# Where the matmul operands begin in SBUF: padded weight slots in a two-layer streaming encoder

## The chip, the cores and the metric

The kernel runs on one NeuronCore of one Trainium2 chip. The metric is the device time of one execution in microseconds. Before the change three runs took 1301.45, 1302.26 and 1303.33 us; the median is 1302.26. The profile is of one further execution, which took 1301.85 us; its span from the first to the last instruction is 1300.1 us, and 1.75 us lie around that span.

## The reference

A sequence of 512 frames with 1024 features goes through two layers. Layer 0 mixes with an RWKV-7 recurrence beside attention into 256 memory tokens; layer 1 mixes with chunked attention beside memory attention. Each mixer is followed by an output projection and by a gated feed-forward block with a short convolution. All arithmetic is float32.

```python
def conv_glu(h, w_in, conv_w, conv_b, w_out):        # D_FF = 2816, CONV_W = 3
    seq = h.shape[1]
    gate, val = jnp.split(h @ w_in, 2, axis=-1)
    gp = jnp.pad(gate, ((0, 0), (CONV_W - 1, 0), (0, 0)))
    conv = conv_b + sum(conv_w[j] * gp[:, j:j + seq] for j in range(CONV_W))
    return (jax.nn.gelu(conv, approximate=False) * val) @ w_out

for layer in range(DEPTH):                            # DEPTH = 2
    h = rms_norm(x, ln1[layer])
    p = h @ w_in_of_the_layer
    mix = rwkv7_time_mix(...) if layer == 0 else chunk_attention(...)
    mo = memory_attention(q_mem, mem_n, w_mem_kv[layer])
    x = x + jnp.concatenate([mix, mo], axis=-1) @ w_out[layer]
    x = x + conv_glu(rms_norm(x, ln2[layer]), ffn_in[layer], ffn_conv[layer],
                     ffn_conv_b[layer], ffn_out[layer])
return rms_norm(x, ln_f)
```

## The kernel before

**Products.** Every large product is made of three matmuls on float32r operands. A float32 operand is split into a high part (a copy rounded to float32r, on ScalarE, ACT) and a low part (the remainder, a subtraction on VectorE, DVE, or a negated copy on ACT with a DMA that adds the source, issued by GpSimd, POOL). The three are high by high, high by low, and low by high. Each matmul has 128 stationary columns ("weights") and a moving operand of 512 or of 256 columns, and each brings its own weight load.

**Weight slots.** The pool `wp` holds raw weights (`wraw`, 2 slots), high parts (`whi`, 3 slots) and low parts (`wlo`, 3 slots), each 1024 float32 columns a partition, 4096 bytes. `split_w`, `raw_w` and `load_w` (L172 to L198) fill them. `wlv` is one more low part that shares the slots of `wraw`.

**512-wide products.** `dense` (L213) has the weights in `whi`/`wlo` and a 512-wide activation moving: `r1h`/`r1l` in layer 0's projections, in layer 0's output projection, in layer 1's key projections (`k_proj`) and in the last tile of layer 1's feed-forward input; `r2h`/`r2l` in the corresponding places of the other layer. `rows` (L652, matmuls on L658 and L663) computes the feed-forward output with the activations stationary (`r1h`, `r1l`, `r2h`, `r2l`, `th`, `tl`, `sl`) and the 512-wide chunks of `whi`/`wlo` moving.

**256-wide products.** The feed-forward input projection takes 21 of its 22 tiles by a seven-product scheme on half-size blocks: class `Seven`, one `frame` (L506) a tile, whose seven calls of `prod` (L408, matmuls on L414 and L416) make 7 x 12 = 84 matmuls, each with a 256-wide moving operand out of `Uh`/`Ul` (3 products) or `Th`/`Tl` (4 products) and weights out of `whi`, `wlo` or `wlv`. `U` is `r2h`/`r2l` in layer 0 and `r1h`/`r1l` in layer 1; `T` is `th`/`tl` in both. While PE works on tile j, DVE and ACT build the sums and splits of tile j + 1 and finish tiles j - 1 and j - 2. Inside the frames every DVE and ACT instruction stands in a written order (`keep`). `v_proj` (L1711) has 256-wide weights moving and `r1h`/`r1l` stationary.

**The order around them.** In the mixer stages generators of instructions are woven by cost (`weave`, L87); the feed-forward stages are written out by hand. The tile framework adds all waits: a new tile in a slot waits for the last reader of the old one.

**Places.** The allocator puts tiles of a pool one behind the other and rounds each up to 32 bytes. `cst` begins 16,512 bytes into a partition; it has 710 columns (2840 bytes, rounded to 2848), `vec` 316 columns (1264, rounded to 1280), and `r1h` follows at 20,640. This gives, in the built program, as bytes past a multiple of 256:

| tiles | bytes past a multiple of 256 |
|---|---|
| `r1h`, `r1l`, `acc`, `rho` | 160 |
| `wraw`, `wlv`, `whi`, `wlo` (all slots), `tmp` | 128 |
| `r2h`, `r2l`, `th`, `tl`, `sl`, `raw`, `sp`, `xT` | 128 |

Inside these tiles an operand begins at a multiple of 512 bytes (128 weight columns) or of 1024 or 2048 (256 or 512 moving columns), so an operand has the place of its tile.

Of the kernel before, what the change touches and what calls it, by code (L numbers as in the profile page):

```python
# [112 lines left out]
        e[3] = now + wait  # L113


@with_exitstack
def trunk_kernel(ctx, tc, A, out):
    nc = tc.nc
# [1 line left out]
    cp = ctx.enter_context(tc.tile_pool(name="cp", bufs=1))  # L120
    wp = ctx.enter_context(tc.tile_pool(name="wp", bufs=3))
    dp = ctx.enter_context(tc.tile_pool(name="dp", bufs=1, space=bass.MemoryType.DRAM))
    banks = {}

    def open_banks(stack, **n):
# [3 lines left out]

    open_banks(ctx, D=2)  # L130
    cst = cp.tile([P, NCST], F32, name="cst")
    vec = cp.tile([P, NVEC], F32, name="vec")
    r1h = cp.tile([P, KD, S], F32R, name="r1h", tag="r1h")
    r1l = cp.tile([P, KD, S], F32R, name="r1l", tag="r1l")
    acc = cp.tile([P, S], F32, name="acc")
    rho = cp.tile([P, S], F32, name="rho")
    rc = cp.tile([P, 4], F32, name="rc")

    def C(name, lo=0, n=None):
        o, w = COFF[name]  # L140
# [28 lines left out]
    lo_on = [0]  # L169
    raw_at = [None]  # L170

    def split_w(raw, n, src=None, pin=lambda i: i, first=False, hold=False):  # L172
        hi = wp.tile([P, 1024], F32R, name="whi", tag="whi")
        lo = wp.tile([P, 1024], F32R, name="wlo", tag="wlo")
        high = lambda: pin(SC.copy(hi[:, :n], raw))  # L175

        def low():
            if src is not None:

                pin(SC.activation(lo[:, :n], raw, AF.Copy, scale=-1.0))  # L180
                GP.dma_start(lo[:, :n], src, accum_op=ALU.add)
            else:
                pin(V.tensor_tensor(lo[:, :n], raw, hi[:, :n], op=ALU.subtract))  # L183

        first, second = (low, high) if first else (high, low)
        first()
        if hold:
            return hi, lo, second
        second()
        return hi, lo  # L190

    def raw_w(src, n=1024):
        raw = wp.tile([P, 1024], F32, name="wraw", tag="wraw", bufs=2)
        raw_at[0] = nc.sync.dma_start(raw[:, :n], src)
        return raw[:, :n]

    def load_w(src, n=1024, lo=None):
        return split_w(raw_w(src, n), n, src if (lo_on[0] if lo is None else lo) else None)  # L198

    def mm3(ps, wh, wl, ah, al, start, stop):  # L200
        PE.matmul(ps, wh, ah, start=start, stop=False)
# [195 lines left out]
    def ffn(l, hp, U, T, new_x, xT, after=None, tokens=None):  # L397
# [29 lines left out]
        class Seven:  # L427
# [18 lines left out]
                    GP.dma_start(low[:], self.second[:, n], accum_op=ALU.add)  # L446

            def rest(self):
                self.low = wp.tile([P, 1024], F32R, name="wlv", tag="wraw", bufs=2)
                keep(SC.activation(self.low[:], self.pair(G2), AF.Copy, scale=-1.0))  # L450
                GP.dma_start(self.low[:].rearrange("p (a s) -> p a s", a=2), self.second, accum_op=ALU.add)  # L451

# [11 lines left out]
                keep(V.tensor_tensor(raw[:, S4], raw[:, S2], raw[:, G2], op=ALU.add))  # L464

            def high(self, what, n=1024):
                hi = wp.tile([P, 1024], F32R, name="whi", tag="whi")
                keep(SC.copy(hi[:, :n], self.pair(what) if n > S else self.raw[:, what]))  # L468
                return hi

            def lower(self, what, hi, n=1024):
                lo = wp.tile([P, 1024], F32R, name="wlo", tag="wlo")
                keep(V.tensor_tensor(lo[:, :n], self.pair(what) if n > S else self.raw[:, what], hi[:, :n], op=ALU.subtract))  # L473
                return hi, lo

# [30 lines left out]
            def frame(self, prev2, prev, nxt, norm=None, ending=None):  # L506
                first = prev is None
                if nxt:
                    nxt.load()
                f1, f2, f3, self.f4 = (ps_f() for _ in range(4))  # L510
                g = self.g = tmp()
                prod(f1[:, h1], (self.gs, 0), XU(0, 0))
                if first:
                    hv = self.hv
                    self.h31 = self.high(S3)
                else:
                    hv = self.high(G2)
                keep(SC.copy(g[:, h1], f1[:, h1]))
                if first:
                    prod(self.f4[:, h1], ((hv, self.lows[0]), 0), XU(1, 0), True)  # L520
                if norm and not first:
                    run(norm)
                w31 = self.lower(S3, self.h31)
                if prev:
                    prev.end1()
                    prev.endr()
                prod(f2[:, h1], (self.gs, S), XT(T2), first)
                w4 = self.lower(S4, self.high(S4, S), S)
                if nxt and prev:
                    prev.end2()  # L530
                    prev.endt()
                elif prev:
                    next(ending)
                    next(ending)
                keep(V.tensor_tensor(g[:, h2], g[:, h1], f2[:, h1], op=ALU.subtract))  # L535
                if nxt and prev:
                    prev.end3()
                    prev.endd()
                if nxt:
                    nxt.sums()  # L540
                    nxt.sum2()
                    nxt.rest()
                if nxt and prev2:
                    prev2.end4()
                    prev2.end5()
                c = self.c = tmp()
                prod(f1[:, h2], (w31, 0), XT(T3))
                keep(V.tensor_tensor(c[:, h1], f1[:, h2], g[:, h2], op=ALU.subtract))
                if first:
                    next(norm)  # L550
                prod(f3[:, h2], (w31, S), XT(T1))
                if nxt:
                    nxt.gs = nxt.lower(G1, nxt.high(G1))
                    nxt.sum4()
                else:
                    next(ending)
                if first:
                    next(norm)
                v = self.v = tmp()
                prod(f3[:, h1], ((hv, self.lows[1]), S, 0) if first else ((hv, self.low), S), XT(T4))  # L560
                keep(V.tensor_tensor(v[:].rearrange("p (a s) -> p a s", a=2), c[:, h1].unsqueeze(1).to_broadcast([P, 2, 256]),
                                     f3[:].rearrange("p (a s) -> p a s", a=2), op=ALU.add))
                keep(V.tensor_tensor(g[:, h2], g[:, h2], f3[:, h2], op=ALU.subtract))
                if nxt:
                    nxt.h31 = nxt.high(S3)
                else:
                    next(ending)
                if not first:
                    prod(self.f4[:, h1], ((hv, self.low), 0), XU(1, 0))
                prod(self.f4[:, h2], (w4, 0), XU(1, 1))  # L570
# [69 lines left out]
        def chunk(raw, c, spare=False):  # L640
            n = 2 if c < 3 else 1
            s_ = raw[:, 2 * c:2 * c + n].rearrange("p k s -> p (k s)")
            if spare and c > 1:
                hi, lo = (t[:, 2 * c - 4:2 * c - 4 + n].rearrange("p k s -> p (k s)") for t in (Th, Tl))
            else:
                hi = wp.tile([P, 1024], F32R, name="whi", tag="whi")[:, :n * S]
                lo = wp.tile([P, 1024], F32R, name="wlo", tag="wlo")[:, :n * S]
            SC.copy(hi, s_)  # L648
            V.tensor_tensor(lo, s_, hi, op=ALU.subtract)  # L649
            return hi, lo, n  # L650
# [233 lines left out]
        return ap.unsqueeze(1).to_broadcast([P, 8, 64])  # L884

    def lora_load(idx):
        raw = wp.tile([P, 1024], F32, name="wraw", tag="wraw", bufs=2)
        nc.sync.dma_start(raw[:], A["lora"][idx])
        return raw

# [2 lines left out]
    xs = [Tt3[:, 0:2].rearrange("p m c t -> p m (c t)"),  # L893
          kt_("MQ", (P, 8, 128))[:].rearrange("p a b -> p (a b)").rearrange("p (m s) -> p m s", m=2)]
    xs += [flat(kt_("AR", (P, NCH, 2, 64), bufs=2), 2) for _ in range(2)]
    lraw = wp.tile([P, 1024], F32, name="wraw", tag="wraw", bufs=2)
    for m in range(KD):
        nc.sync.dma_start(xs[m // 2][:, m % 2], A["xT"][:, m])
        if m in (0, 2):
            u = slice(m * 256, m * 256 + 512)  # L900
            nc.sync.dma_start(lraw[:, u], A["lora"][0][:, u])
    nc.sync.dma_start(vec[:, 24:], A["vec"][:, 24:])
    kraw = wp.tile([P, 1024], F32, name="wraw", tag="wraw", bufs=2)
    nc.sync.dma_start(kraw[:], A["wA"][1])
    nc.sync.dma_start(cst, A["cst"])

# [13 lines left out]

    def lora_split(idx, raw, parts=1):

        hi, lo = zip(*((wp.tile([P, 1024], F32R, name="whi", tag="whi"), wp.tile([P, 1024], F32R, name="wlo", tag="wlo"))
                       for _ in range(2)))
        mraw = flat(kt_("KB", (P, NCH, 3, 64), bufs=2), 1)[:, 0, 0:1024]
        r3 = raw[:].rearrange("p (k f) -> p k f", k=8)
        m3 = mraw.rearrange("p (k f) -> p k f", k=8)
# [565 lines left out]
    def lora_one():  # L1493

        with tc.issue_after(norm_at[0].ins):
            *_, lw_ = lora_split(1, lora_load(1))
        yield from lora_pair(1, *lw_)


    lora0 = lora_pair(0, *lw)  # L1500
# [6 lines left out]
    GP.memset(acc[:], 1.0)  # L1507
    GP.memset(acc[:, 0:S:64], 0.0)
    run(lora0)
    first = prepare(0, Ts[0])  # L1510
    for _ in range(5):
        next(first)
# [130 lines left out]
    with ExitStack() as bctx:  # L1643
# [67 lines left out]
        def v_proj(g, wv=None):  # L1711
            yield lambda: g < 2 or 2 * g - 3 in done
            vS[g] = ap_.tile([P, 4, 256], F32, name="vS", tag="vS")
            wv = wv or [load_w(A["w_kvv"][g, u]) for u in range(2)]
            for t2 in range(2):

                pp_ = ps_d() if g else ps_s()
# [77 lines left out]
        run(dense(pq[1][:], [(first[1], K8)], act2, order=K8[4:8], start=False))  # L1795
        next(norm)
        run(dense(pk[:], [(wk, K8)], act1, order=K8[4:8], start=False))
        wv = [load_w(A["w_kvv"][0, u]) for u in range(2)]
        run(norm)
        for i in range(2):  # L1800
            q_split(pq[i], Tb[i])
# [187 lines left out]
```

## Time and profile before

| | us | share of the span |
|---|---|---|
| median of three runs | 1302.26 | |
| profiled execution | 1301.85 | |
| its span | 1300.1 | |
| PE busy (10,420 matmuls) | 1278.6 | 98% |
| PEld busy (weight loads) | 1100.9 | 85% |
| ACT busy | 836.5 | 64% |
| POOL busy | 137.6 | 11% |

The stages follow one another: layer 0's mixer up to about 388 us, the feed-forward frames of layer 0 from 388 to 603 us, its output from 613 to 727, layer 1's mixer from 727 to 953, the frames of layer 1 from 953 to 1166, its output from 1177 to the end. Matmuls are pipelined and their ends are modelled, so neighbouring matmuls overlap in the profile and the busy share of PE says little; the distance between the starts of two neighbours says what one costs. The chain of waits merges neighbouring matmuls of one line into a piece, with their count and the time from the first start to the start of what follows, and so shows this distance.

### The profile page before, as it was taken

What the parts mean: (1) busy time and instruction counts of PE and PEld (TensorE: products, weight loads), DVE (VectorE), ACT (ScalarE), POOL (GpSimd) and SP (SyncE); (2) the same over time, 40 slices, a digit from 0 to 9 for tenths busy, and PEclk for the clock granted to TensorE, in tenths of its full rate; (3) what the DMA queues carried; (4) which work ended last, traced back from release to release, by engine and by line L of the source; (5) the groups of instructions that cost most, each with busy time, mean ns of one, the idle gap of its engine ahead of it and who ended that gap; (6) DMA issues with size and microseconds to landing.
All of it is one profiled execution on the core that took longest, in us unless ns stands there. A gap on an engine that the chain in (4) does not pass through costs nothing.

```text
span 1300.1 us, 26329 instructions
## 1 busy us (share of the span) xinstructions
PE 1278.6 (98%) x10420; PEld 1100.9 (85%) x10420; DVE 1041.8 (80%) x1956; ACT 836.5 (64%) x1380; POOL 137.6 (11%) x164
## 2 busy tenths in 40 slices
PE   9999999999999999999999999999999999999997
PEld 7887777777789999999888878787799999998886
DVE  7967767775589999999876876658889999998684
ACT  6666767756566666767554676657757666665562
POOL 1000000000001112110220000000011122111200
PEclk9999999999999999999999999999999999999999
DMA  6365434452236777886984332223437878879951
GB/s 202 110 177 116 112 69 106 95 113 69 82 114 148 182 175 193 189 183 176 270 179 122 123 90 85 81 95 115 130 80 183 183 173 197 186 159 285 214 141 65
DMA packets 92988, 187.42 MB, mean 144 GB/s; under 512 B 21824, under 2 KB 30144, under 8 KB 92864
## 3 DMA queue, kind: packets, MB, share of 16 engines
q1 hardware_dynamic: 68592, 129.14, 31.1%
q0 software_dynamic: 24272, 56.59, 25.0%
q8 instruction: 82, 1.34, 0.4%
q14 instruction: 42, 0.34, 0.1%
HBM read 169.48 MB, written 6.29 MB: 135 GB/s over the span
## 4 chain that ended last, share of the span: by engine, by line
PE 83%; DVE 7%; ACT 6%; issue 1%; DMA 1%; SPq 0%; ACTq 0%; DVEq 0%
PE psf L414 21%; PE psf L416 11%; PE psf L658 7%; PE psd L225 6%; PE psd L221 6%; PE psd L222 5%; PE psf L663 4%; PE psd L658 3%; PE psd L663 2%; PE pss L1774 1%; PE pss L658 1%; DVE wlo L183 1%; PE pss L1404 1%; PE pss L350 1%; PE pss L1760 1%
## 5 line engine op out<-in xcount | busy, mean ns | idle before, releaser
L468 ACT CAST whi<-raw 128x1024 fp32r<-128x1024 f32 (+1 forms) x168 | 151.8, 941 | 66.2 <-PE psf L414 37.4
L414 PE MATMUL psf<-tl,whi 128*128 128x256 f32 x672 | 168.6, 283 | 0.0
L414 PE MATMUL psf<-th,whi 128*128 128x256 f32 x672 | 168.3, 283 | 0.0
L473 DVE TENSOR_TENSOR wlo<-raw,whi 128x1024 fp32r<-128x1024 f32 (+1 forms) x126 | 131.5, 1043 | 14.3 <-ACT whi L468 14.2
L175 ACT CAST whi<-wraw 128x1024 fp32r<-128x1024 f32 x84 | 87.7, 1047 | 69.3 <-PE psd L222 36.1
L414 PEld LDWEIGHTS psf<-tl,whi 128*128 128x128 f32 x672 | 128.7, 192 | 0.0
L414 PEld LDWEIGHTS psf<-th,whi 128*128 128x128 f32 x672 | 128.5, 192 | 0.0
L221 PE MATMUL psd<-r1h,whi 128*128 128x512 f32 x264 | 108.2, 410 | 0.0
L222 PE MATMUL psd<-r1l,whi 128*128 128x512 f32 x264 | 105.6, 401 | 0.0
L183 DVE TENSOR_TENSOR wlo<-wraw,whi 128x1024 fp32r<-128x1024 f32 x65 | 79.3, 1219 | 15.9 <-ACT whi L175 13.6
L648 ACT CAST whi<-raw 128x1024 fp32r<-128x1024 f32 (+1 forms) x52 | 49.6, 954 | 65.2 <-PE psf L658 35.4
L649 DVE TENSOR_TENSOR wlo<-raw,whi 128x1024 fp32r<-128x1024 f32 (+1 forms) x52 | 56.7, 1099 | 42.6 <-ACT whi L648 33.6
L416 PE MATMUL psf<-th,wlo 128*128 128x256 f32 x504 | 81.2, 283 | 0.0
L225 PE MATMUL psd<-r1h,wlo 128*128 128x512 f32 x264 | 74.9, 405 | 0.0
L416 PEld LDWEIGHTS psf<-th,wlo 128*128 128x128 f32 x504 | 69.7, 192 | 0.0
L451 POOL DMA_DIRECT2D wlv<-in_ffn_in_dram x40 | 61.2, 1530 | 59.7 <-DVE tmp L535 58.7
L494 ACT ACTIVATE tmp<-tmp,vec 128x512 f32<-128x512 f32 x44 | 35.9, 817 | 47.3 <-DVE tmp L481 47.1
L414 PE MATMUL psf<-r2h,whi 128*128 128x256 f32 x252 | 63.3, 283 | 0.5 <-ACT whi L468 0.5
L414 PE MATMUL psf<-r2l,whi 128*128 128x256 f32 x252 | 63.2, 283 | 0.0
L414 PE MATMUL psf<-r1h,whi 128*128 128x256 f32 x252 | 62.5, 281 | 0.5 <-ACT whi L468 0.5
L414 PE MATMUL psf<-r1l,whi 128*128 128x256 f32 x252 | 62.1, 279 | 0.0
L221 PEld LDWEIGHTS psd<-r1h,whi 128*128 128x128 f32 x264 | 49.5, 188 | 13.0 <-issue 2.5
(608 smaller groups left out, 3545.7 us busy)
## 6 DMA issues: line engine op xcount, KB each, us to landing
raw<-in_ffn_in_dram SPq DMA_DIRECT2D x42, 512.0 KB, 3.8
raw<-in_ffn_in_dram SPq DMA_DIRECT2D x84, 256.0 KB, 4.2
wlv<-in_ffn_in_dram POOLq DMA_DIRECT2D x40, 512.0 KB, 8.0
raw<-in_ffn_out_dram SPq DMA_DIRECT2D x30, 512.0 KB, 5.9
raw<-in_ffn_out_dram POOLq DMA_DIRECT2D x24, 512.0 KB, 8.0
wraw<-in_wA_dram SPq DMA_DIRECT2D x20, 512.0 KB, 4.2
wraw<-in_w_out_dram SPq DMA_DIRECT2D x16, 512.0 KB, 3.9
wraw<-in_ffn_outp_dram SPq DMA_DIRECT2D x16, 512.0 KB, 4.7
```

Source lines behind the costliest of these rows:

```text
L175: high = lambda: pin(SC.copy(hi[:, :n], raw))
L183: pin(V.tensor_tensor(lo[:, :n], raw, hi[:, :n], op=ALU.subtract))
L221: PE.matmul(ps, wh[:, j * P:(j + 1) * P], ah, start=start and n == 0, stop=False)
L222: dense_at[0] = PE.matmul(ps, wh[:, j * P:(j + 1) * P], al, start=False, stop=False)
L225: dense_at[0] = PE.matmul(ps, wl[:, j * P:(j + 1) * P], act(k)[0], start=False, stop=stop and n == len(ks) - 1)
L414: PE.matmul(ps, wh[:, o + k * P:o + k * P + P], x[k][n], start=k == n == 0, stop=False)
L416: PE.matmul(ps, wl[:, ol + k * P:ol + k * P + P], x[k][0], start=False, stop=k == 3)
L451: GP.dma_start(self.low[:].rearrange("p (a s) -> p a s", a=2), self.second, accum_op=ALU.add)
L468: keep(SC.copy(hi[:, :n], self.pair(what) if n > S else self.raw[:, what]))
L473: keep(V.tensor_tensor(lo[:, :n], self.pair(what) if n > S else self.raw[:, what], hi[:, :n], op=ALU.subtract))
L658: PE.matmul(ps[:], a[:, k0 + i, ts], hi[:, i * S:i * S + S], start=bool(first) and (first is True or t in first) and a is act[0] and i == ...
L663: PE.matmul(ps[:], act[0][:, k0 + i, ts], lo[:, i * S:i * S + S], start=False, stop=bool(last) and t in last and i == n - 1)
```

## The change

No instruction is added or taken out. Tiles get other places:

- `vec` gets 28 more columns and `rc` 8 more (both are cut back to their old width by a slice). This moves `r1h` and `r1l` on by 96 bytes, and all that follows `rc` by 128.
- A weight slot is 1056 columns, 4224 bytes, instead of 1024. `wtile` hands out a part of it: from column 0 or, for `wlo`, from column 32 (128 bytes).
- `whi` and `wlo` no longer are one tag with three buffers each but three tags each (`whi0` to `whi2`, `wlo0` to `wlo2`) with one buffer, taken in turn. The turn skips slots that stand in `held` (the two pairs of the low-rank weights, until their products are done), and is moved on by hand around `h31` of the first frame.
- For weights of 256-wide products (`high`, `lower`, `rest`, and `v_proj`'s loads) the part begins at column 16 (64 bytes).

```diff
+W_AT = {"whi": 0, "wlo": 32}
+W_NARROW = 16
...
+    turns, held = {"whi": 0, "wlo": 0}, set()
+
+    def wtile(name, dt=F32R, tag=None, at=None):
+        if name in turns:
+            n = turns[name]
+            while (name, n) in held:
+                n = (n + 1) % 3
+            turns[name] = (n + 1) % 3
+            tag = f"{name}{n}"
+            at = W_AT[name] if at is None else at
+        else:
+            at = at or 0
+        t = wp.tile([P, 1056], dt, name=name, tag=tag or name, bufs=1 if name in turns else 2)
+        return t[:, at:at + 1024]
...
-    vec = cp.tile([P, NVEC], F32, name="vec")
+    vec = cp.tile([P, NVEC + 28], F32, name="vec")[:, :NVEC]
...
-    rc = cp.tile([P, 4], F32, name="rc")
+    rc = cp.tile([P, 12], F32, name="rc")[:, :4]
...
-    def split_w(raw, n, src=None, pin=lambda i: i, first=False, hold=False):
-        hi = wp.tile([P, 1024], F32R, name="whi", tag="whi")
-        lo = wp.tile([P, 1024], F32R, name="wlo", tag="wlo")
+    def split_w(raw, n, src=None, pin=lambda i: i, first=False, hold=False, at=None):
+        hi = wtile("whi", at=at)
+        lo = wtile("wlo", at=at)
...
-        raw = wp.tile([P, 1024], F32, name="wraw", tag="wraw", bufs=2)
+        raw = wtile("wraw", F32)
...
-                self.low = wp.tile([P, 1024], F32R, name="wlv", tag="wraw", bufs=2)
+                self.low = wtile("wlv", tag="wraw", at=W_NARROW)
...
-                hi = wp.tile([P, 1024], F32R, name="whi", tag="whi")
+                hi = wtile("whi", at=W_NARROW)
...
-                lo = wp.tile([P, 1024], F32R, name="wlo", tag="wlo")
+                lo = wtile("wlo", at=W_NARROW)
...
                 if first:
                     hv = self.hv
+                    turns["whi"] = (turns["whi"] + 1) % 3
                     self.h31 = self.high(S3)
+                    turns["whi"] = (turns["whi"] + 1) % 3
...
-                hi = wp.tile([P, 1024], F32R, name="whi", tag="whi")[:, :n * S]
-                lo = wp.tile([P, 1024], F32R, name="wlo", tag="wlo")[:, :n * S]
+                hi = wtile("whi")[:, :n * S]
+                lo = wtile("wlo")[:, :n * S]
...
-        hi, lo = zip(*((wp.tile([P, 1024], F32R, name="whi", tag="whi"), wp.tile([P, 1024], F32R, name="wlo", tag="wlo"))
+        hi, lo = zip(*((wtile("whi"), wtile("wlo"))
                        for _ in range(2)))
+        held.update((n_, (turns[n_] + 1 + i_) % 3) for n_ in turns for i_ in range(2))
...
-            wv = wv or [load_w(A["w_kvv"][g, u]) for u in range(2)]
+            wv = wv or [load_w(A["w_kvv"][g, u], at=W_NARROW) for u in range(2)]
```

The other uses of `wraw`, `whi` and `wlo` are replaced by `wtile` in the same way, and `held` is cleared after each pair of low-rank products.

More of the change, by code (lines that the diff above doesn't have):

```diff
@@ L192, in raw_w, with load_w @@
     def raw_w(src, n=1024):
-        raw = wp.tile([P, 1024], F32, name="wraw", tag="wraw", bufs=2)
+        raw = wtile("wraw", F32)
         raw_at[0] = nc.sync.dma_start(raw[:, :n], src)
         return raw[:, :n]
-    def load_w(src, n=1024, lo=None):
-        return split_w(raw_w(src, n), n, src if (lo_on[0] if lo is None else lo) else None)
+    def load_w(src, n=1024, lo=None, at=None):
+        return split_w(raw_w(src, n), n, src if (lo_on[0] if lo is None else lo) else None, at=at)
     def mm3(ps, wh, wl, ah, al, start, stop):
@@ L886, in lora_load @@
     def lora_load(idx):
-        raw = wp.tile([P, 1024], F32, name="wraw", tag="wraw", bufs=2)
+        raw = wtile("wraw", F32)
         nc.sync.dma_start(raw[:], A["lora"][idx])
@@ L895, in trunk_kernel @@
     xs += [flat(kt_("AR", (P, NCH, 2, 64), bufs=2), 2) for _ in range(2)]
-    lraw = wp.tile([P, 1024], F32, name="wraw", tag="wraw", bufs=2)
+    lraw = wtile("wraw", F32)
     for m in range(KD):
@@ L902, in trunk_kernel @@
     nc.sync.dma_start(vec[:, 24:], A["vec"][:, 24:])
-    kraw = wp.tile([P, 1024], F32, name="wraw", tag="wraw", bufs=2)
+    kraw = wtile("wraw", F32)
     nc.sync.dma_start(kraw[:], A["wA"][1])
@@ L1497, in lora_one @@
         yield from lora_pair(1, *lw_)
+        held.clear()
     lora0 = lora_pair(0, *lw)
@@ L1509, in trunk_kernel @@
     run(lora0)
+    held.clear()
     first = prepare(0, Ts[0])
@@ L1797, in trunk_kernel @@
         run(dense(pk[:], [(wk, K8)], act1, order=K8[4:8], start=False))
-        wv = [load_w(A["w_kvv"][0, u]) for u in range(2)]
+        wv = [load_w(A["w_kvv"][0, u], at=W_NARROW) for u in range(2)]
         run(norm)
```

## The prediction

> **What bounds the kernel now.** I read the page first, then the stages' busy times, then the chain of waits inside stages that hold matmuls of one kind only.
>
> ```profile
> PE 1278.6 (98%) x10420; PEld 1100.9 (85%) x10420; DVE 1041.8 (80%) x1956; ACT 836.5 (64%) x1380; POOL 137.6 (11%) x164
> PE 83%; DVE 7%; ACT 6%; issue 1%; DMA 1%; SPq 0%; ACTq 0%; DVEq 0%
> ```
>
> PE carries 83% of the chain that ended last, so the distance between neighbouring matmuls is what the time is made of. Two pairs of pieces of the chain give that distance: first 512-wide in the two output stages (layer 0, then layer 1), then 256-wide in the two runs of frames (layer 0, then layer 1).
>
> ```profile
> 644.75 1.81 PE pss L658 x8
> ...
> 1206.03 1.87 PE pss L658 x8
> ```
>
> ```profile
> 412.49 0.96 PE psf L414 x8
> 413.45 0.48 PE psf L416 x4
> ...
> 1004.33 0.94 PE psf L414 x8
> 1005.27 0.47 PE psf L416 x4
> ```
>
> One 512-wide matmul costs 1.81/8 = 0.2267 us in layer 0 and 1.87/8 = 0.2333 in layer 1: same line, same shape, same clock, 6.6 ns apart. One 256-wide costs 120 ns in layer 0 and (0.94 + 0.47)/12 = 118 ns in layer 1, the other way round. The mean durations show the same by operand (they are some 163 ns longer than the distance, because neighbours overlap):
>
> ```profile
> L658 PE MATMUL pss<-whi,r1l 128*128 128x512 f32 x28 | 7.2, 396 | 0.0
> L658 PE MATMUL pss<-whi,r2l 128*128 128x512 f32 x28 | 7.0, 389 | 0.0
> L414 PE MATMUL psf<-tl,whi 128*128 128x256 f32 x336 | 84.2, 283 | 0.0
> L414 PE MATMUL psf<-r1l,whi 128*128 128x256 f32 x252 | 62.1, 279 | 0.0
> ```
>
> `tl` and `r1l` stand in the same frames of layer 1, with the same weights, and still differ by 4 ns, so it isn't the stage. What differs is the place: `r1h`/`r1l` begin 160 bytes past a multiple of 256, everything else named here 128. I call the distance between the places of the moving operand and of the weights, modulo 128, the offset. Offset 0: 226.7 and 120.0 ns. Offset 32: 233.3 and 118 ns. A half-line shift costs a wide product 6.6 ns and saves a narrow one 2.
>
> The second bound stands close behind the frames:
>
> ```profile
> 410.00:580.00 170.00, 170.00 (x1419) 170.00 (x1418) 162.96 (x238) 118.69 (x155) 36.50 (x35) 1.00 0.80 185
> 975.00:1145.00 170.00, 170.00 (x1427) 169.87 (x1427) 162.92 (x239) 117.68 (x155) 36.49 (x34) 1.00 0.80 184
> ```
>
> The columns are PE, PEld, DVE, ACT, POOL. A frame has 84 matmuls: 170/1419 x 84 = 10.06 us in layer 0, 170/1427 x 84 = 10.01 in layer 1. DVE is busy 95.9% of that, 9.65 us a frame.
>
> **The change, part by part.** `r1h`/`r1l` go from 160 + 96 to 0, everything behind `rc` from 128 + 128 to 0. A slot of 4224 bytes is 16.5 times 256, so slots follow each other 0, 128, 0, 128; with `wlo` beginning 128 bytes in, all wide operands land on 0. Narrow weights land on 64 (`whi`) and 192 (`wlo`), offset 64 from activations on 0.
>
> *Wide products, offset 32 to 0.* Those with `r1h`/`r1l`, counted in the loops of the code: 252 in layer 1's output (168 on L658, 84 on L663), and 960 in `dense` (264 on each of three lines into `psd`, 96 into `psl`, 48 into `psf`, 24 into `pss`).
>
> ```profile
> L221 PE MATMUL psd<-r1h,whi 128*128 128x512 f32 x264 | 108.2, 410 | 0.0
> L222 PE MATMUL psd<-r1l,whi 128*128 128x512 f32 x264 | 105.6, 401 | 0.0
> L221 PE MATMUL psd<-r2h,whi 128*128 128x512 f32 x128 | 51.8, 406 | 0.1
> L222 PE MATMUL psd<-r2l,whi 128*128 128x512 f32 x128 | 50.7, 396 | 0.0
> ```
>
> Where PE streams without a break (the 252, the 48 into `psf`, 48 of layer 1's last input tile) each saves 6.6 ns: 348 x 6.6 = 2.3 us. In the mixers, where other work stands between, the rows with `r1` are only 4 to 5 ns longer than those with `r2`; I take 4.1: 864 x 4.1 = 3.5 us. Together 5.8. That offset 0 is worth the same on 0 as on 128 is not shown; the bounds are the 106 ns that 256 more columns take (389 - 283) as the whole cost of a half, 212, and today's worst, 233.3. I take 226.7, because it is the same at every multiple of 512 bytes inside the slots.
>
> *Narrow products in the frames, offset 0 or 32 to 64.* No row shows offset 64. From below: 106 ns, as above, with nothing on top. From above: 120 plus the 6.6 that a wide product pays at a wrong place, 127. Two ways of going on from the rows, another 2 ns for the second half line (116) or one step of 6.6 down from 120 (113), give PE 84 x 0.116 = 9.74 or 84 x 0.113 = 9.5 us a frame; below 9.65 DVE takes over, and some of its waits stay:
>
> ```profile
> L473 DVE TENSOR_TENSOR wlo<-raw,whi 128x1024 fp32r<-128x1024 f32 (+1 forms) x45 | 46.9, 1043 | 4.3 <-ACT whi L468 4.3
> ```
>
> 4.3 us over 15 frames is 0.3 a frame, a wait for ACT's cast, which itself waits for PE to free the slot; with PE earlier it shrinks. So anything from 113 to 116 ns ends at about 9.75 us. That is my value: (10.06 - 9.75) x 21 = 6.5 us in layer 0 and (10.01 - 9.75) x 21 = 5.5 in layer 1, 12.0 in all. What is late next is DVE: `wlo` of the next tile, and PE behind it.
>
> *Narrow products in `v_proj`.* 288, offset 32 to 64, with `r1` as weights:
>
> ```profile
> L1725 PE MATMUL psd<-whi,r1l 128*128 128x256 f32 x64 | 18.1, 283 | 0.0
> L1726 PE MATMUL psd<-wlo,r1h 128*128 128x256 f32 x64 | 17.8, 281 | 0.0
> ```
>
> At 2 ns each, 0.6 us. The memory weights keep column 0 and their old offset.
>
> *DVE, ACT and loads.* Their operands move too. DVE's time doesn't depend on place so far: `L504` writes `sp` (place 128) and in layer 0 `r1l` (place 160) in the same time, so I add nothing.
>
> ```profile
> L504 DVE TENSOR_TENSOR sp<-tmp 128x512 f32<-128x512 f32 x7 | 4.8, 685 | 0.9 <-ACT tmp L501 0.9
> L504 DVE TENSOR_TENSOR r1l<-tmp 128x512 f32<-128x512 f32 x7 | 4.8, 684 | 0.0
> ```
>
> *Slots in turn.* No instruction comes or goes. The three buffers were already used in rotation; the two turns by hand give `h31` the slot of the last output-projection weights and the next weights that of the first frame's gate sum, both free by then. The cost is nothing, covered by the matmuls that ACT's casts already wait for. If a slot were still read, a cast (0.94 us) and a subtraction (1.04) would come late once a layer, about 4 us in all. DVE's low part of the first frame's fourth sum may wait for the second product, but the next DVE instruction waits for it anyway.
>
> The sum: 5.8 + 12.0 + 0.6 = 18.4 us off the profiled 1301.85, 1283.4; the median of the runs lies 0.4 above the profiled one, so 1284.
>
> **The rivals.**
>
> *Only the half line counts for narrow products* (64 costs what 32 does, 118 ns). Layer 0's frame becomes 84 x 0.118 = 9.91, saving 0.15 x 21 = 3.2; layer 1 gains only on its 48 products with `th`/`tl`, 48 x 2 ns x 21 = 2.0. With 5.8 that is 11.0: 1291. For it: it is the nearest row. Against: nothing.
>
> *The pattern repeats every 64 bytes* (64 costs what 0 does, 120). Layer 1 loses 36 x 2 ns x 21 = 1.5, `v_proj` 0.6; 5.8 - 2.1 = 3.7: 1298.5. Against: wide and narrow react oppositely to 32, so the place within a longer run matters.
>
> *Narrow products pay at 64 what wide ones pay at 32*: 120 + 6.7 = 127 ns. A frame is 84 x 0.127 = 10.67, plus 0.61 and 0.66 over 21 frames each, 26.7; `v_proj` 288 x 9 ns = 2.6; less 5.8: about 1325, slower. It decides from some 121 ns on, where 3528 narrow matmuls eat the 5.8. For it: a wide product does react upward to a shift. Against: the narrow ones went down with the first 32 bytes.
>
> *Place does nothing.* [...] The trace disagrees where `tl` and `r1l` differ inside one frame. As a mechanism of this kernel (the two rows differ by which stage wrote or reads the tiles): 1302.
>
> **How the numbers follow.** Forecast 0.45, with its own range 1279 to 1288; half line only 0.20; period of 64 bytes 0.13; narrow products dearer 0.13; nothing 0.06; still faster, because wide products on 0 cost under 226.7 or DVE's waits vanish, 0.03. About 0.2% (2.6 us) is what a measurement of this kernel can tell from no change, so faster means below 1299.7: 0.45 + 0.20 + 0.10 (of the 64-byte rival) + 0.03 = 0.78; within, 0.03 + 0.06 = 0.09; slower, 0.13. The range 1276 to 1304 leaves out the dear rival and the best case, 0.16.
>
> **What would show it.** Pieces of the chain in the output stage of layer 1 should take 1.81 us for 8 matmuls. In the frames, neighbours 113 to 116 ns apart, now with gaps before `wlo` or `whi`, and DVE over 98% busy; the frames of both layers equally long. Layer 0's output and `r2` projections unchanged. If narrow matmuls are 120 or more apart in the frames, or the wide ones stay at 233, the forecast is wrong at that step; a new wait of ACT for PE at the first frame would show the slots at fault.

## The result and the profile after

| | before | after |
|---|---|---|
| median of 22 runs each, us | 1302.69 | 1299.85 |
| lowest to highest | 1300.96 to 1304.44 | 1299.03 to 1301.41 |
| span of the profiled execution | 1300.1 | 1297.5 |

The ratio is 0.998, 95% interval 0.9974 to 0.9987: faster by 2.8 us, where 18 were forecast. In the changed file the matmuls of `prod` are on L433 and L435 (before L414 and L416), those of `rows` on L679 and L684 (L658, L663), those of `dense` on L240, L241 and L244 (L221, L222, L225); inside a frame's loop all lines are 19 to 21 further.

Pieces of the chain of waits after the change, first in the output stage of layer 1, then in the frames of layer 0 (start, us, what):

```profile
1201.91 1.81 PE pss L679 x8
```

```profile
469.04 1.06 ACT whi L487
...
470.12 1.24 DVE wlo L492
...
471.40 0.74 PE psf L435 x4
...
473.52 0.91 PE psf L433 x8
474.42 0.45 PE psf L435 x4
```

Both prices came as forecast: 1.81/8 = 226 ns for a wide product, (0.91 + 0.45)/12 = 113 ns for a narrow one. What is new stands between them: ACT's cast, then DVE's subtraction, then PE. At 113.4 ns (as experiment 5 has it) a frame's 84 matmuls take 9.53 us. They should make up the whole frame, and don't. Busy times in the same stretches as before (PE, PEld, DVE, ACT, POOL):

```profile
410.00:580.00 170.00, 168.17 (x1431) 164.82 (x1430) 162.93 (x239) 117.65 (x155) 36.48 (x34) 1.00 0.80 184
975.00:1145.00 170.00, 169.29 (x1431) 165.44 (x1430) 162.92 (x239) 117.66 (x155) 36.47 (x34) 1.00 0.79 185
```

170/1431 x 84 = 9.98 us a frame, against 10.06 and 10.01. DVE did 239 instructions in 170 us, as before (238 and 239): its pace did not change. The page after the change, its chain by engine:

```profile
PE 71%; DVE 13%; ACT 9%; DMA 4%; issue 3%; SPq 0%; ACTq 0%; DVEq 0%
```

On the chain PE fell from 83% to 71%, and DVE rose from 7% to 13%.

Where the 2.6 us of the spans come from is read from the first and last starts (us) of two groups of matmuls in each layer: `psf<-...,wlo` in the frames, `psf<-whi,th` in the output. Before:

```profile
L416 PE MATMUL psf<-r2h,wlo x168: 277/283/365, 389.3 to 602.3; 128*128 128x256 f32 x168
L658 PE MATMUL psf<-whi,th x48: 389/389/395, 613.3 to 713.6; 128*128 128x512 f32 x48
L416 PE MATMUL psf<-r1h,wlo x168: 277/280/379, 953.9 to 1165.6; 128*128 128x256 f32 x168
L658 PE MATMUL psf<-whi,th x48: 389/389/395, 1176.9 to 1280.2; 128*128 128x512 f32 x48
```

After:

```profile
L435 PE MATMUL psf<-r2h,wlo x168: 276/276/392, 388.9 to 599.8; 128*128 128x256 f32 x168
L679 PE MATMUL psf<-whi,th x48: 389/389/395, 612.4 to 712.7; 128*128 128x512 f32 x48
L435 PE MATMUL psf<-r1h,wlo x168: 276/277/393, 952.5 to 1163.2; 128*128 128x256 f32 x168
L679 PE MATMUL psf<-whi,th x48: 389/389/395, 1175.9 to 1277.7; 128*128 128x512 f32 x48
```

| stage | how read | before | after | difference |
|---|---|---|---|---|
| mixer, layer 0 | start of the frames | 389.3 | 388.9 | -0.4 |
| frames, layer 0 | last less first | 213.0 | 210.9 | -2.1 |
| last input tile, layer 0 | output's first less frames' last | 11.0 | 12.6 | +1.6 |
| output of layer 0 and mixer of layer 1 | to the next frames' first | 340.6 | 340.1 | -0.5 |
| frames, layer 1 | last less first | 211.7 | 210.7 | -1.0 |
| last input tile, layer 1 | | 11.3 | 12.7 | +1.4 |
| output, layer 1 | last less first | 103.3 | 101.8 | -1.5 |

The output of layer 1 gave 1.5 us, nearly the 1.7 of 252 products at 6.6 ns. The frames gave 3.1 of 12.0, and the last input tile behind them took 3.0 back.

### The profile page after: what moved, and what is told of

Read it like the earlier page. It is cut to its first block, busy times and chain, and to the rows that moved or that the text cites. A ratio compares the mean times of both kernels' runs of the same rounds, so it can differ in the third digit from the quotient of the medians.

```text
span 1297.5 us, 26319 instructions
## 1 busy us (share of the span) xinstructions
PE 1269.0 (98%) x10420; PEld 1086.4 (84%) x10420; DVE 1040.7 (80%) x1956; ACT 835.9 (64%) x1380; POOL 137.5 (11%) x164
## 4 chain that ended last, share of the span: by engine, by line
PE 71%; DVE 13%; ACT 9%; DMA 4%; issue 3%; SPq 0%; ACTq 0%; DVEq 0%
PE psf L433 13%; PE psf L435 8%; PE psf L679 7%; PE psd L244 6%; PE psd L240 5%; PE psd L241 5%; PE psf L684 4%; PE psd L679 3%; DVE wlo L492 3%; ACT whi L487 3%; PE psd L684 2%; PE pss L1798 1%; DMA wraw<-in_ffn_in_dram 1%; PE pss L679 1%; DVE wlo L202 1%
## 5 line engine op out<-in xcount | busy, mean ns | idle before, releaser
L433 PE MATMUL psf<-tl,whi 128*128 128x256 f32 x672 | 161.3, 276 | 0.0
L433 PE MATMUL psf<-th,whi 128*128 128x256 f32 x672 | 161.2, 277 | 0.0
L194 ACT CAST whi<-wraw 128x1024 fp32r<-128x1024 f32 x84 | 87.7, 1048 | 75.7 <-PE psd L241 36.6
L433 PEld LDWEIGHTS psf<-tl,whi 128*128 128x128 f32 x672 | 126.0, 188 | 0.0
L433 PEld LDWEIGHTS psf<-th,whi 128*128 128x128 f32 x672 | 125.9, 188 | 0.0
L240 PE MATMUL psd<-r1h,whi 128*128 128x512 f32 x264 | 107.4, 407 | 0.0
L241 PE MATMUL psd<-r1l,whi 128*128 128x512 f32 x264 | 105.0, 398 | 0.0
L435 PE MATMUL psf<-th,wlo 128*128 128x256 f32 x504 | 78.2, 277 | 0.0
L244 PE MATMUL psd<-r1h,wlo 128*128 128x512 f32 x264 | 74.2, 403 | 1.1 <-DMA wlo<-in_ffn_in_dram 0.9
L435 PEld LDWEIGHTS psf<-th,wlo 128*128 128x128 f32 x504 | 66.7, 188 | 0.0
L433 PE MATMUL psf<-r2h,whi 128*128 128x256 f32 x252 | 62.0, 282 | 1.2 <-ACT whi L487 1.1
L433 PE MATMUL psf<-r1h,whi 128*128 128x256 f32 x252 | 61.9, 282 | 0.7 <-ACT whi L487 0.7
L433 PE MATMUL psf<-r1l,whi 128*128 128x256 f32 x252 | 60.8, 277 | 0.0
L433 PE MATMUL psf<-r2l,whi 128*128 128x256 f32 x252 | 60.7, 277 | 0.0
L240 PEld LDWEIGHTS psd<-r1h,whi 128*128 128x128 f32 x264 | 49.5, 188 | 11.9 <-issue 2.1
```

Source lines behind the costliest of these rows:

```text
L240: PE.matmul(ps, wh[:, j * P:(j + 1) * P], ah, start=start and n == 0, stop=False)
L241: dense_at[0] = PE.matmul(ps, wh[:, j * P:(j + 1) * P], al, start=False, stop=False)
L244: dense_at[0] = PE.matmul(ps, wl[:, j * P:(j + 1) * P], act(k)[0], start=False, stop=stop and n == len(ks) - 1)
L433: PE.matmul(ps, wh[:, o + k * P:o + k * P + P], x[k][n], start=k == n == 0, stop=False)
L435: PE.matmul(ps, wl[:, ol + k * P:ol + k * P + P], x[k][0], start=False, stop=k == 3)
```

## Why the frames stopped at 9.96 us

DVE's instructions in one frame, before the change (start, duration, and in brackets its idle time and who ended it):

```profile
500.51 1.23 DVE L473 TENSOR_TENSOR wlo<-raw,whi 128x1024 fp32r<-128x1024 f32 x1 [0.31 <-ACT whi L468]
...
508.54 0.69 DVE L460 TENSOR_TENSOR raw<-raw 128x512 f32<-128x512 f32 x1
509.14 0.68 DVE L504 TENSOR_TENSOR r1l<-tmp 128x512 f32<-128x512 f32 x1
509.75 0.42 DVE L548 TENSOR_TENSOR tmp<-psf,tmp 128x256 f32<-128x256 f32 x1
510.47 1.23 DVE L473 TENSOR_TENSOR wlo<-raw,whi 128x1024 fp32r<-128x1024 f32 x1 [0.31 <-ACT whi L468]
```

After:

```profile
500.01 1.23 DVE L492 TENSOR_TENSOR wlo<-raw,whi 128x1024 fp32r<-128x1024 f32 x1 [0.31 <-ACT whi L487]
...
508.03 0.69 DVE L479 TENSOR_TENSOR raw<-raw 128x512 f32<-128x512 f32 x1
508.64 0.68 DVE L523 TENSOR_TENSOR r1l<-tmp 128x512 f32<-128x512 f32 x1
509.25 0.42 DVE L569 TENSOR_TENSOR tmp<-psf,tmp 128x256 f32<-128x256 f32 x1
509.97 1.23 DVE L492 TENSOR_TENSOR wlo<-raw,whi 128x1024 fp32r<-128x1024 f32 x1 [0.31 <-ACT whi L487]
```

The same subtraction comes round after 510.47 - 500.51 = 9.96 us before and 509.97 - 500.01 = 9.96 us after. In each turn DVE is idle for 0.31 us before it, for ACT's cast of the same blocks. And what does that cast wait for? The waits between 410 and 580 us before the change (total, times, longest) name two:

```profile
ACT whi L468 <- PE psf L414: 14.2, 26, 1.2
ACT whi L468 <- DVE raw L460: 10.2, 14, 0.8
DVE wlo L473 <- ACT whi L468: 5.5, 16, 0.9
```

Fourteen of the seventeen frames have the second: ACT waits for DVE's own sum of the blocks (L460). That sum ends at 508.54 + 0.69 = 509.23, the cast takes about 1.06 us (the chain above), and the subtraction starts at 510.47; between sum and subtraction DVE has only two other instructions to do. After the change the profile names a matmul of PE for most of these casts and the sum for three only, where a matmul ends at nearly the same moment. The distance decides: in every frame but the first behind 410 and behind 975 us, before and after the change, the cast starts 0.85 to 0.86 us after the start of the sum, wherever PE's matmuls stand. So the wait belongs to DVE's own order, PE has no part in it, and DVE's loop was 9.96 us long beside PE's 10.06. I call this theory D: place made PE faster as forecast, and DVE's loop of 9.96 us kept the frame there. It says that a single move, the fourth sum (`sum4`) into that gap, sets the rest of the gain free, and only together with the new places.

## The experiments

**1. The fourth sum into the gap, on both kernels.** The first on the changed kernel, the second on the kernel before:

```diff
-                    nxt.gs = nxt.lower(G1, nxt.high(G1))
-                    nxt.sum4()
+                    g1 = nxt.high(G1)
+                    nxt.sum4()
+                    nxt.gs = nxt.lower(G1, g1)
```

> The changed kernel, with the next tile's fourth sum put ahead of the low part of its gate weights on DVE, so that DVE works while ACT casts. Theory D (DVE's own loop of 9.96 us sets the frames; 0.31 us of it is a wait for a cast that itself waits for DVE's second sum): the loop falls to about 9.65 us, 42 frames save some 12 us, total about 1288 (ratio to before 0.988). Theory M (the DMA traffic of the frames sets 9.96): no difference to the changed kernel, about 1300. Theory S (the new slots or their turns ate the gain on PE or ACT): no difference, about 1300.

> The kernel before, with the same reordering on DVE. Theory D: PE paces the frames there at 10.08 and 10.00 us, so the shorter DVE loop is idle time; 0 to 3 us less than before, the most of it at the end of the frames. Theory that DVE already set the frames before: 4 to 12 us less.

On the changed kernel: 1284.99 us (1284.28 to 1285.66), ratio 0.9862 [0.9849, 0.9876]. On the kernel before: 1301.98 (1301.24 to 1302.4), ratio 0.9992 [0.9983, 1.0001]. DVE in the first, with the wait between 410 and 560 us behind it:

```profile
496.34 1.22 DVE L492 TENSOR_TENSOR wlo<-raw,whi 128x1024 fp32r<-128x1024 f32 x1
...
504.96 0.42 DVE L569 TENSOR_TENSOR tmp<-psf,tmp 128x256 f32<-128x256 f32 x1
505.30 0.68 DVE L483 TENSOR_TENSOR raw<-raw 128x512 f32<-128x512 f32 x1
505.90 1.22 DVE L492 TENSOR_TENSOR wlo<-raw,whi 128x1024 fp32r<-128x1024 f32 x1
```

```profile
DVE wlo L492 <- ACT whi L487: 0.3, 1, 0.3
```

```profile
L435 PE MATMUL psf<-r2h,wlo x168: 276/276/393, 388.6 to 592.4; 128*128 128x256 f32 x168
L435 PE MATMUL psf<-r1h,wlo x168: 276/276/388, 944.8 to 1149.2; 128*128 128x256 f32 x168
```

The sum (L483) fills the gap, the wait is gone, and the frames take 203.8 and 204.4 us: 9.2 and 7.3 less than before the change. DVE's turn is now 505.90 - 496.34 = 9.56 us. That is 0.40 less, where 0.31 was expected, and so the time is 1285 and not 1288: without the wait the next instruction here starts 0.08 us before the end of the one ahead (505.30, where 504.96 + 0.42 is 505.38), and the wait had cost that overlap too. The same edit alone, with PE still at 118 to 120 ns, gains nothing that can be told from zero. Rivals in which something other than DVE's order held the frames (M and S) fall with this pair.

**2. The fourth sum left out** of the changed kernel (`-                    nxt.sum4()`).

> The changed kernel with the fourth sum left out (its block keeps the raw weights). Theory D: DVE's loop 9.96 - 0.60 = 9.36 us, below PE's 84 x 113.5 ns = 9.53; frames at 9.5 to 9.6, 42 x 0.4 = 17 us less than the changed kernel, about 1283. Theories M and S: about 1300.

1281.45 us (1281.1 to 1282.37), ratio 0.9836 [0.9823, 0.9849]. That is 3.5 us below moving it, 3.5/42 = 0.08 us a frame, for a DVE instruction of 0.68. In that kernel the same subtraction comes round after 9.36 us in the early frames and after 9.52 in the later ones, which is PE's 9.53 (1322 matmuls in the 150 us from 975 us on, 150/1322 x 84 = 9.53). So in the kernel with the moved sum (9.56) DVE is still the nearer bound, but PE stands right behind it.

**3. Only the wide places**, and then the moved sum without the narrow places:

```diff
-W_NARROW = 16
+W_NARROW = 0
```

> The changed kernel with narrow weights at column 0 again (offset 0 to the activations). Theory D: narrow matmuls 120 ns apart again, frames 10.08 us, but the stage from the first frame to the output product within 1 us of before; total within 1.5 us of the changed kernel, because what is left of the gain comes from the wide products. If the narrow places are worth what the frames showed (3 us), total about 1303.

> e1 with narrow weights at column 0 again. Theory D: PE is the bound of the frames there (84 x 120 = 10.08 us against DVE's 9.65), so the narrow places, worth next to nothing in the change as it stands, are worth 42 x 0.42 = 15 to 18 us here: about 1300 to 1302 against e1's 1285. If e1's gain came from DVE alone, without the places: about 1288.

Wide places alone: 1300.83 us (1300.15 to 1302.98), ratio 0.9988 [0.9979, 0.9997]. Moved sum with narrow weights back on 0: 1299.77 (1297.23 to 1302.06), ratio 0.998 [0.997, 0.9989]. With the two runs of experiment 1 this makes a square:

| us | sum where it was | sum in the gap |
|---|---|---|
| kernel before | 1302.69 | 1301.98 |
| new places, narrow weights on 0 | 1300.83 | 1299.77 |
| new places, narrow weights on 64 | 1299.85 | 1284.99 |

Narrow weights on 64 are worth 1.0 us in the left column, where the intervals overlap and it can't be told from nothing, and 14.8 in the right one. (On 0 holds for the high parts. By the slots' places `wlo` then lies 128 bytes past the activations, 118.7 ns in experiment 5, and a frame takes about 10.0 us and not 10.08; the second run came out just under the expected 1300.) The forecast of 12.0 was a price of the right column, paid in the left.

**4. Two more moves in DVE's order**, on top of the moved sum: `prev.endr()` behind `w4`, and `nxt.sums()` ahead of the finishing steps `end3` and `endd`.

```diff
                     prev.end1()
-                    prev.endr()
...
                 w4 = self.lower(S4, self.high(S4, S), S)
+                if prev:
+                    prev.endr()
...
+                if nxt:
+                    nxt.sums()
                 if nxt and prev:
                     prev.end3()
                     prev.endd()
                 if nxt:
-                    nxt.sums()
                     nxt.sum2()
```

> The changed kernel with the fourth sum early as in e1, and two more instructions of DVE moved so that neither follows at once the one whose result it reads (the scaling by rho behind the split of the fourth sum; the second sum behind the convolution's middle tap). Theory D: DVE's loop loses two gaps of 0.115 us more, 9.65 - 0.23 = 9.42, below PE's 84 x 113.5 ns = 9.53; frames at about 9.55, 4 us less than e1, about 1281. If the end of the gate's chain on ACT now comes too late, DVE waits for it and nothing or less than nothing is gained on e1 (1285).

1286.89 us (1286.17 to 1287.24), ratio 0.988 [0.9865, 0.9894]: no better than the one move, and the intervals overlap, so slower isn't shown. Its DVE has a new wait, behind the second sum (L479):

```profile
505.93 0.69 DVE L523 TENSOR_TENSOR r1l<-tmp 128x512 f32<-128x512 f32 x1 [0.24 <-ACT tmp L520]
```

`endr` later makes ACT's gelu (L520) later, and the gap returns at another place.

**5. The cost of places by itself.** In place of the model stand, for each of twelve places (`m`, `w`) and each width `n`, 48 products with new weights at every one, in one run:

```diff
+    for n, m, w in [(512, 0, 0)] + GROUPS:
+        ps = pp.tile([P, S], F32, name="ps", tag="ps")
+        for r in range(EACH):
+            j, k = r % 8, r % 4
+            nc.tensor.matmul(ps[:, :n], wt[:, w // 4 + j * P:w // 4 + j * P + P],
+                             mov[:, m // 4 + k * S:m // 4 + k * S + n], start=r == 0, stop=r == EACH - 1)
```

> Left out: the whole model. 25 runs of 48 matmuls each, 128 weight columns, 512 or 256 moving columns, places of both operands set by hand, nothing else on the chip's engines. If the distance of two neighbours hangs on the offset modulo 128 alone: 512-wide 226.7 ns at offset 0 and 128, 233.3 at 32 and 96; 256-wide 120.0 at 0 and 128, about 118 at 32 and 96, 113.3 at 64; the same for both on 128 or both on 32. If the place itself counts: 128 and 128 differs from 0 and 0, or 32 and 32 does.

Mean distance between the starts of neighbours from the eighth of the 48 on, in ns, by the bytes that each operand lies past a multiple of 256. (The first few after a new place come less evenly, at (128, 128) with up to 236 ns between them.)

| moving, weights | 512 wide | 256 wide |
|---|---|---|
| 0, 0 | 226.7 | 120.0 |
| 128, 128 | 226.8 | 120.0 |
| 32, 32 | 226.9 | 120.0 |
| 0, 16 | 226.7 | 118.3 |
| 0, 32 | 233.3 | 118.3 |
| 0, 48 | 233.3 | 117.9 |
| 0, 64 | 233.3 | 113.3 |
| 0, 96 | 234.3 | 120.0 |
| 0, 128 | 232.4 | 118.7 |
| 128, 0 | 233.4 | 118.7 |
| 64, 0 | 228.9 | 117.8 |
| 32, 0 | 233.3 | 116.7 |

Some of them as pieces of that kernel's chain: wide on (0, 0) and (0, 32), then narrow on (0, 0) and (0, 64).

```profile
26.82 10.20 PE ps L38 x45
...
48.82 10.26 PE ps L38 x44
...
159.92 5.16 PE ps L38 x43
...
182.92 4.65 PE ps L38 x41
```

10.20/45 = 226.7, 10.26/44 = 233.2, 5.16/43 = 120.0, 4.65/41 = 113.4 ns. With nothing else in the kernel but these products, the places alone make the differences: 226.7 to 234.3 ns for a wide one, 113.3 to 120.0 for a narrow one. Equal places cost the same on 0, 32 and 128 (226.7, 226.9 and 226.8; 120.0 each), so there only the distance counts; but not modulo 128, since (0, 128) isn't (0, 0) (232.4 against 226.7, 118.7 against 120.0), and not symmetric, since (0, 64) isn't (64, 0) (233.3 against 228.9, 113.3 against 117.8).

**6. What took 3.0 us back in the last input tile.** The chain after the change, behind the frames of layer 0:

```profile
596.69 0.95 ACT whi L194
...
597.65 6.97 DMA wraw<-in_ffn_in_dram
...
604.70 1.00 ACT whi L194
...
609.25 1.15 DVE wlo L202
...
610.44 2.11 PE psd L244 x8
```

Before the change this stretch was matmuls alone. Now the tile's second raw weights come last: their load starts at 597.65, once the cast of the first (L194) has freed a slot of `wraw`. PE itself sits idle twice in this stretch: 0.8 us for an adding DMA of POOL, which makes the low part of the first weights, and 0.2 us for DVE's subtraction of the second. Two kernels load them at the tile's start into a free slot of `raw`: the first on the changed kernel, the second on that with the moved sum.

```diff
             wg = split_w(raw_w(src[0]), 1024, src[0], keep, True, True)
+            wv_raw = hp.tile([P, 7, S], F32, name="raw", tag="raw", bufs=2)[:, 0:2].rearrange("p a s -> p (a s)")
+            nc.sync.dma_start(wv_raw, src[1])
...
-            wv_raw = raw_w(src[1])
```

> The changed kernel, with the second raw weights of the last input tile loaded at the tile's start into a free slot of `raw` instead of a slot of `wraw` that is still being read. Theory D's part on the last tile: the feed-forward output starts late because this load waits for the slot; with it early, the output starts some 1.4 us earlier in each layer (about 611.0 and 1172.9), in all 2.8 us less: about 1297. Rival: something else holds the last tile (the first weights' low part by POOL's DMA, or ACT's and DVE's work): 1299 to 1300.5, with the output starting where it does now.

> The same load, with the changed kernel in which the fourth sum also stands ahead of the first low part. Theory D: 1284.99 less about 2.8 us, some 1282. Rival (something else holds the last tile): 1284.5 to 1285.5.

1300.25 us (1298.92 to 1302.58), ratio 0.9978 [0.9968, 0.9987], and 1284.43 (1283.9 to 1285.15), ratio 0.9857 [0.9842, 0.9872]. Neither can be told from its parent, and both lie at the rival's numbers. The chain of the first shows why:

```profile
596.80 7.81 DMA wlo<-in_ffn_in_dram
...
604.65 2.11 PE psd L244 x8
```

Beside the load stood a second transfer, that adding DMA of POOL. It lands at 604.61; in the changed kernel the load had landed at 604.62. So two kernels more, with that low part made by DVE, and behind the cast instead of ahead of it:

```diff
-            wg = split_w(raw_w(src[0]), 1024, src[0], keep, True, True)
+            wg = split_w(raw_w(src[0]), 1024, None, keep, False, True)
```

> The kernel of e8_last_tile_load_apart, with the low part of the last tile's first weights made by DVE's subtraction instead of by a negated copy on ACT and an adding DMA of POOL. In e8 that DMA took 7.81 us and landed at 604.61, where before the change PE had its 604.4 or so without a wait; what stands behind the slot is therefore this DMA. Theory: with it gone PE goes through the last tile without a break, the output starts 1 us or more earlier in each layer than in e8 (about 611.0 and 1173.5 or before), some 2 us off 1300.25: 1298. Rival (DVE's own wait and 1.2 us come late in the last frame instead): no gain, 1300 to 1302.

> The same edit on e9_both_edits. Theory: some 2 us off 1284.43: 1282. Rival: 1284 to 1286.

On the changed kernel: 1297.75 us (1297.09 to 1299.77), ratio 0.9964 [0.9952, 0.9977], 2.1 us under the changed kernel's median, though the intervals overlap. PE now runs without a break up to the low part of the tile's second product. The 16 matmuls `psd<-r2h,whi` of its two products (8 each) from first to last start, before and after the change and in this kernel:

```profile
L221 PE MATMUL psd<-r2h,whi x16: 389/389/396, 602.4 to 611.0; 128*128 128x512 f32 x16
```

```profile
L240 PE MATMUL psd<-r2h,whi x16: 389/389/395, 599.9 to 609.6; 128*128 128x512 f32 x16
```

```profile
L240 PE MATMUL psd<-r2h,whi x16: 389/389/395, 601.3 to 610.0; 128*128 128x512 f32 x16
```

8.6, 9.7 and 8.7 us. Taking the slot's wait away alone gained nothing that shows; with both taken away PE's break is gone. (The low part by DVE with the load left in its slot was not tried.) With the moved sum the last edit gives 1284.75 (1284.48 to 1286.35), ratio 0.9862 [0.9847, 0.9878], no gain: there PE arrives so early that the first load itself (8.34 us, landing at 591.60) is what comes last in the chain, and DVE's subtraction behind it. In the profiled execution, the longest of its four, PE also waits 1.9 us in layer 0, in two waits, for adding DMAs of `wlv`.

How much of the 3.0 us comes from PE being earlier stays open. In the kernel with only the wide places (experiment 3) the frames end no earlier than before the change, and the last input tile still takes 12.5 us in layer 0 (from the two groups of matmuls below) and 11.9 in layer 1, where it had taken 11.0 and 11.3:

```profile
L435 PE MATMUL psf<-r2h,wlo x168: 274/281/367, 389.9 to 602.5; 128*128 128x256 f32 x168
L679 PE MATMUL psf<-whi,th x48: 389/389/395, 615.0 to 715.4; 128*128 128x512 f32 x48
```

The transfers differ from trace to trace: POOL's adding DMA took 5.5 and 7.2 us from issue to landing in the two layers before the change, 7.4 and 7.4 after it, 7.3 and 7.4 in this kernel; layer 0's load of the second raw weights took 5.7, 7.0 and 6.8.

The fastest version that keeps the whole computation is the changed kernel with the moved sum, at 1284.43 to 1284.99 us with or without the load apart.

## Why the prediction was right or wrong

**Wide products: right where PE streams.** 226 ns instead of 233 in the output of layer 1, -1.5 us where 252 x 6.6 ns are 1.7; and with these places alone (experiment 3) the ratio is 0.9988, or 1.6 us, though its interval runs from 0.4 to 2.7.

**Wide products in the mixers: mis-sized.** The term 864 x 4.1 ns = 3.5 us measured about 0.9 (0.4 and 0.5 in the table of stages), and the 0.4 is not told from chance: in the other kernels with the new wide places the frames of layer 0 start between 388.1 and 390.2 us. The rows over the whole program fell by 3 ns, not by 4:

```profile
L240 PE MATMUL psd<-r1h,whi 128*128 128x512 f32 x264 | 107.4, 407 | 0.0
L241 PE MATMUL psd<-r1l,whi 128*128 128x512 f32 x264 | 105.0, 398 | 0.0
```

410 and 401 were read as place alone against the 406 and 396 of `r2`, though the two stand among different work; and a mixer need not end 3 ns earlier because a matmul in it does, when what it waits for comes from other engines. That last part is argued from the stage's total; no run took it apart.

**Narrow products in the frames: the price right, the step behind it wrong.** The value chosen was 113 to 116 ns, measured 113.4. These were two ways of going on from two rows, and no run says why the step of 6.6 ns was the right one: the number was in part luck. The step that failed is this one: "4.3 us over 15 frames is 0.3 a frame, a wait for ACT's cast, which itself waits for PE to free the slot; with PE earlier it shrinks. So anything from 113 to 116 ns ends at about 9.75 us". The cast waited for DVE's own sum, so the 0.31 stayed, and the bound was DVE's turn from one start to the next, 9.96, not its busy time, 9.65. The rows to see it stood in the profile before: the second waiting line of L468, and two starts of L473 in a row. 12.0 us became 3.1. Experiments 1 to 3 show it: removing that one wait brings the kernel to 1284.99, 1 us from the forecast number, by a step the change doesn't contain.

**What is late next: half right.** "DVE: `wlo` of the next tile, and PE behind it" is what the chain shows at 470.12. That the last input tile could wait for its transfers was not considered; in these traces it cost 3.0 us, nearly all that the frames had gained. How much of it comes from PE's lead stays open (experiment 6). DVE "over 98% busy" came only with the moved sum, here between 410 and 560 us:

```profile
410.00:560.00 150.00, 149.68 (x1309) 149.06 (x1308) 148.04 (x220) 107.75 (x143) 32.19 (x30) 1.00 0.83 190
```

148.04/150 = 98.7%, and 95.8% without it.

**`v_proj`: wrong, small.** 0.6 us assumed that offsets work both ways. There the weights move and `r1` stands, so the high parts go from the pair 0, 32 to the pair 64, 0: by experiment 5 from 118.3 to 117.8 ns. The rows after the change agree; 283 and 281 ns stood before:

```profile
L1749 PE MATMUL psd<-whi,r1l 128*128 128x256 f32 x64 | 18.1, 283 | 0.0
L1750 PE MATMUL psd<-wlo,r1h 128*128 128x256 f32 x64 | 17.7, 279 | 0.0
```

Nothing for the high parts, 2 ns for the low ones, which is a third of the products: 96 x 2 ns = 0.2 us.

**Slots in turn, at nothing.** No run has the new slots without the new places, so the price of this part alone was not tried.

**The rivals.** Half line only (118 ns at 64; "half line" is the prediction's word for 32 bytes, no run shows a line), the 64-byte period (120) and narrow products dearer (127) all fall by the 113.3 of experiment 5. Yet three rivals named times nearer than the forecast's 1284 (half line 1291, 64-byte period 1298.5, "Place does nothing" 1302), for reasons that fell: place does a great deal (14.8 us in the right column of experiment 3), and DVE's turn and the last tile's transfers hide it. "Place does nothing" is answered by experiment 5: the moving operand stays where it is, only the weights' place changes, and a narrow product goes from 120.0 to 113.3 ns.

## What to carry to other kernels

Before pricing a faster engine, measure the turn of the next engine in the loop from start to start, its waits included, and follow each of these waits to the instruction it really ends on: busy time (here 9.65 us a frame) says how short the loop could be, not how short it will be (here 9.96). A wait between two engines that both lie off the path can be the next bound, and moving one independent instruction into it may be worth more than the change itself, though alone, as here, it is worth nothing that can be measured. And where a stage gets ahead, look at what must land for the next one.

## What the runs showed of the hardware

In experiment 5 the cost of a float32r product with new weights each time went with how far apart its two operands lie, and the best distance with its width: of the twelve pairs tried, 512 columns are best at equal places or with the weights 16 bytes past (226.7 against up to 234.3 ns), 256 columns with the weights 64 bytes past the moving operand (113.3, against 120.0 at equal places). The best value and the common worse one lie 6.6 and 6.7 ns apart (233.3 and 120.0). Why the distance matters, and why width turns its sign, stays open; so does any pair but these twelve. (In the frames `wlo` lies 192 past the activations, and the chain shows 0.45/4 = 113 ns there too.)
